# Compressed keys and values of the last three chunks of the sparse branch made in one pass

## The chip, the cores and the metric

The kernel runs on one core of one Trainium2 chip. The metric is the device time of one execution in microseconds (us). All numbers are of the kernel before the change: its runs, and one execution that was profiled.

## The reference

One pre-norm decoder layer: 2048 tokens of width 1024, an input projection of 2700 columns, four attention groups A (stick-breaking), B (native sparse), C (differential) and D (sliding window with sinks), an output projection, an MLP of width 4096 with squared ReLU, and a final norm. The part that the change touches is the compression of group B's keys and values:

```python
def compress(t, pe, w1, w2):                       # 127 windows of 32 tokens, 16 apart, per tensor
    blk = (t[:, idx] + pe).reshape(B, n_cmp, CMP_LEN * t.shape[-1])
    return jax.nn.gelu(blk @ w1) @ w2

kc = compress(k_cmp, pe_k, w1_k, w2_k)
vc = compress(v_cmp, pe_v, w1_v, w2_v)
z = einsum('bthd,bid->bhti', q, kc) * scale - slopes * dist_c     # masked where dist_c < 0
p_c = softmax(z) * valid_c
o_cmp = einsum('bhti,bid->bthd', p_c, vc)
imp = einsum('bhti,ij->btj', p_c, to_sel)          # picks 8 blocks of 64 keys: o_sel
o_nsa = g0 * o_cmp + g1 * o_sel + g2 * o_win
...
mix = concat(rmsnorm(o_sb), rmsnorm(o_nsa), o_diff, rmsnorm(o_swa))
x = x + (mix * g_mix) @ w_out
h = rmsnorm(x); u = relu(h @ w_up); x = x + (u * u) @ w_down
return rmsnorm(x)
```

## The kernel before, in words

**Chunks and phases.** The tokens are cut into NC = 4 chunks of 512. There are eight dense phases, one after the other: P0 to P3 (`proj`, the input projection of a chunk; its column groups come in the order of the table ORDER, one list for chunk 0 and one for the rest) and M0 to M3 (`mlp`: output projection, MLP and final norm of a chunk). Results of P go to scratch memory in DRAM: `qk_d`, `v_d`, and `kvc_d` for the 64 key and 64 value columns that are to be compressed (the group "kvcmp").

**Attention.** Beside the dense phases run the four groups of each chunk, in the order A, C, D, B, for chunk 0 to 3 (`scores`, line 1028). They work tile by tile of 128 queries; PSUM and transposes of them have names by group and chunk, such as zD, tD, oD in group D (scores, transposes, products with v). Their outputs, normed, are stored to `mix_d`, and `mlp` loads them as the tile nx, 4 tiles of 128 rows a chunk, for its output projection.

**Who sets the order.** Every engine executes its instructions in the order in which they were issued. `run` (line 1537) has ten generators, which stand for the streams of work: weights, splits of weights into a high and a low part, loads, finals, values, compressions, scores, fills and the dense phases. At each step it takes the first stream that could start on TensorE (PE) without waiting, by a plan of costs that it keeps (`Plan`, line 122). All DMAs are issued by SyncE (SP) through `dma` (line 245), and a DMA that waits for its buffer holds up those behind it. Ten names are counted resources (line 224); of `row`, work buffers of 128 x 1024 float32, there are RB = 7, and a stream waits until enough are free.

**Compression.** `compressions` (line 1212) makes the 32 compressed keys and values of chunk c when `scores` arrives at group D of that chunk (`compress_due`); group B of the chunk waits for it (`compressed`, line 1294). `compress(c)` (line 1219) takes 3 rows for as long as it runs: `tmp` and, for key (j = 0) and value (j = 1), one that holds the source from `kvc_d`, on 128 partitions (64 columns of two successive half windows), and beside it the source plus the positional offsets `pet`, reordered so that position l of all 32 windows lies together (line 1242). The offsets are loaded with 4 bytes an element. Then come two rounds of two more rows for the weights `w1t`; in each, 8 positions l, a matmul for key and one for value:

```python
for j in range(2):
    self.mm(ph[64 * j:64 * j + 64], ts[j][:, 32 * l:32 * l + 64],
            w1t[j][:, 128 * l8:128 * l8 + 128], l == 0, l == 15, share=2)
```

The stationary operand is 64 columns wide, of which 32 are windows of this chunk; key and value write the two halves of PSUM's partitions. In the order below such a matmul stands as zD<-row 64x128. After it come GELU on a 128 x 128 tile, a transpose, a small product for the keys (into `kcs`, as a high and a low part) and one for the values (into `vcn`). The lists name the same buffers `row` throughout.

Of the kernel before, what the change touches and what calls it, by code (L numbers as in the profile page):

```python
# [9 lines left out]
F32 = mybir.dt.float32  # L10
F32R = mybir.dt.float32r
U32 = mybir.dt.uint32
AF = mybir.ActivationFunctionType
OP = mybir.AluOpType
# [51 lines left out]

# [131 lines left out]
class Trunk:  # L198
# [1013 lines left out]
    def compressions(self):  # L1212
        for c in range(NC):
            while self.compress_due <= c:
                yield None
            yield from self.compress(c)
            self.compressed = c + 1

    def compress(self, c):


        V, A = self.V, self.A
        yield from self.await_stored("kvcmp", c)
        tmp, *ts = yield from self.rows(3)
# [4 lines left out]
        for j in range(2):  # L1229
            t = ts[j]  # L1230
            src = t[:, 512:1024]
            if c:
                self.ld(src[0:64], self.kvc_d[64 * j:64 * j + 64, 512 * c - 16:512 * c + 496])
            else:
                V.memset(src[0:64, 0:16], 0.0)
                self.ld(src[0:64, 16:512], self.kvc_d[64 * j:64 * j + 64, 0:496])
            self.ld(src[64:128], self.kvc_d[64 * j:64 * j + 64, 512 * c:512 * c + 512])
            self.ld(w2t[j], dap(w2s[j], 0, [[64, 128], [1, 64]]))
# [27 lines left out]
        A.activation(xh, ph, AF.Copy)  # L1266
        V.tensor_tensor(u, xh, xh, OP.mult)
        V.tensor_scalar(u, u, 0.044715, 1.0, op0=OP.mult, op1=OP.add)
        V.tensor_tensor(u, u, xh, OP.mult)
        V.tensor_scalar(u, u, -2.0 * math.sqrt(2.0 / math.pi), 80.0, op0=OP.mult, op1=OP.min)  # L1270
        A.activation(u, u, AF.Exp)
        V.tensor_scalar(u, u, 1.0, None, op0=OP.add)
        V.reciprocal(u, u)
        V.tensor_tensor(xh, xh, u, OP.mult)
        yield self.when([xh], "t", TB)
        pT = self.tt()[:, 0, :]
        self.tr(pT, xh)
        self.evac(xT, pT)
        cs = slice(32 * c, 32 * c + 32)
        yield self.z_when(xT)  # L1280
# [7 lines left out]
        A.activation(self.vcn[cs, :], pv[0:32, 0:64], AF.Copy)  # L1288
        self.give_rows(3)

    def sparse(self, c, pa):
# [330 lines left out]
```

## Time and profile before

| what | value |
|---|---|
| median of 3 runs | 3118.82 us (3118.58 to 3120.22) |
| the profiled execution, its own time | 3114.77 us |
| its span on the core | 3113.0 us, 51339 instructions |
| PE, PE's weight loads | 3010.9 us (97%), 2518.6 us (81%) |
| VectorE (DVE), ScalarE (ACT), GpSimd (POOL) | 1852.3 us (60%), 1563.6 us (50%), 498.8 us (16%) |
| DMA | 566.88 MB, 413690 packets, mean 182 GB/s |

How to read it: the share of busy time is of the span. Matmuls are pipelined, so a record lasts longer than the distance from its start to the next one's; what PE spends on one is that distance. PEld are the weight loads, which lie beside PE's matmuls. The clock is what was granted of 2.4 GHz.

### The profile page before, as it was taken

The numbers are of one execution on the slowest core, as the hardware profiler recorded it, in microseconds if no ns is written. First come the engines' busy times: TensorE is split into PE (matmuls) and PEld (weight loads), VectorE is DVE, ScalarE is ACT, GpSimd is POOL, SyncE is SP. The second block draws the span as 40 slices with busy tenths as digits, with TensorE's granted clock in tenths as the row PEclk, the third lists the DMA queues.
The fourth block names the chain that finished last, engine by engine and source line by source line (L and its number), as shares of the span: only waits on it lengthen the run. The fifth ranks groups of instructions, "written<-read, shape, count | busy, mean of one in ns | idle before, by whom it ended". The sixth has DMA issues, their size and how long they took to land.

```text
span 3113.0 us, 51339 instructions
## 1 busy us (share of the span) xinstructions
PE 3010.9 (97%) x19088; PEld 2518.6 (81%) x19088; DVE 1852.3 (60%) x4157; ACT 1563.6 (50%) x3204; POOL 498.8 (16%) x445
## 2 busy tenths in 40 slices
PE   8999998999999999999999999999999999999998
PEld 7878887888887778878888778879888888888887
DVE  4764667655667887684656776677545553332323
ACT  4754667644656775653646775455434343221111
POOL 3142322323212222230100000011000000110000
PEclk9999999999999999999999999999999999999999
DMA  7768565668366667867235446556743333645554
GB/s 212 197 179 216 155 173 144 191 169 259 135 209 208 200 216 250 253 220 243 96 133 161 139 136 193 172 176 204 209 162 124 124 137 137 237 163 203 183 208 157
DMA packets 413690, 566.88 MB, mean 182 GB/s; under 512 B 132864, under 2 KB 300928, under 8 KB 411776
## 3 DMA queue, kind: packets, MB, share of 16 engines
q1 hardware_dynamic: 413440, 563.60, 56.9%
q8 instruction: 151, 2.47, 0.3%
q14 instruction: 99, 0.81, 0.1%
HBM read 434.41 MB, written 129.07 MB: 181 GB/s over the span
## 4 chain that ended last, share of the span: by engine, by line
PE 73%; DVE 10%; ACT 6%; DMA 5%; issue 3%; SPq 2%; POOL 1%; DVEq 0%; ACTq 0%; POOLq 0%
PE pdM L296 43%; PE pdP L296 9%; DVE row L117 7%; ACT row L117 4%; PE tB L300 4%; PE zB L296 4%; PE oB L296 4%; PE oC L296 2%; PE tC L300 2%; PE zC L296 2%; SPq L252 2%; DVE acc L117 1%; DMA raw<-in_w_in_dram 1%; PE zD L296 1%; PE oA L296 1%
## 5 line engine op out<-in xcount | busy, mean ns | idle before, releaser
L117 DVE TENSOR_TENSOR acc<-acc,pdM 128x512 f32<-128x512 f32 (+1 forms) x576 | 371.1, 653 | 193.7 <-PE pdM L296 184.4
L296 PE MATMUL pdM<-T_hi,w_hi 128*128 128x512 f32 (+1 forms) x936 | 357.6, 383 | 2.7 <-ACT T_hi L117 1.9
L296 PE MATMUL pdM<-T_lo,w_hi 128*128 128x512 f32 (+1 forms) x936 | 358.1, 383 | 1.6 <-POOL T_lo L117 1.6
L296 PE MATMUL pdM<-T_hi,w_lo 128*128 128x512 f32 (+1 forms) x936 | 357.8, 382 | 0.0
L296 PE MATMUL pdM<-w_hi,u_hi 128*128 128x512 f32 x776 | 310.9, 403 | 10.4 <-DVE acc L117 5.6
L296 PE MATMUL pdM<-w_hi,u_lo 128*128 128x512 f32 x776 | 305.7, 394 | 3.8 <-DVE u_lo L117 3.8
L296 PE MATMUL pdM<-w_lo,u_hi 128*128 128x512 f32 x776 | 305.9, 394 | 0.9 <-POOL w_lo L117 0.9
L117 POOL TENSOR_TENSOR w_lo<-raw,w_hi 128x1024 fp32r<-128x1024 f32 (+2 forms) x92 | 225.0, 2449 | 408.9 <-ACT w_hi L117 335.2
L117 ACT ACTIVATE row<-row 128x1024 f32<-128x1024 f32 (+7 forms) x292 | 229.7, 802 | 108.2 <-DVE row L117 101.7
L117 ACT ACTIVATE r<-pdM 128x512 f32<-128x512 f32 x128 | 76.1, 594 | 381.4 <-PE pdM L296 370.1
L117 DVE TENSOR_TENSOR u_lo<-r,u_hi 128x512 fp32r<-128x512 f32 x128 | 93.2, 728 | 285.0 <-ACT u_hi L117 285.0
L117 ACT ACTIVATE w_hi<-raw 128x1024 fp32r<-128x1024 f32 (+2 forms) x160 | 164.7, 1036 | 108.6 <-DMA raw<-in_w_in_dram 48.5
L117 ACT ACTIVATE PT<-tB 128x512 f32<-128x512 f32 (+1 forms) x244 | 130.5, 556 | 170.3 <-PE tB L300 169.5
L117 ACT ACTIVATE row<-row,c_mn 128x1024 f32<-128x1024 f32 (+4 forms) x192 | 171.5, 895 | 87.0 <-DVE c_mn L117 85.2
L296 PEld LDWEIGHTS pdM<-T_hi,w_hi 128*128 128x128 f32 x936 | 175.8, 188 | 35.7 <-ACT T_hi L117 2.3
L296 PEld LDWEIGHTS pdM<-T_lo,w_hi 128*128 128x128 f32 x936 | 176.1, 188 | 34.1 <-POOL T_lo L117 2.1
L296 PEld LDWEIGHTS pdM<-T_hi,w_lo 128*128 128x128 f32 x936 | 176.1, 188 | 32.0 <-issue 0.5
L296 PE MATMUL pdM<-raw,u_hi 128*128 128x512 f32 x496 | 190.0, 391 | 0.0
L296 PE MATMUL pdP<-T_hi,w_hi 128*128 128x512 f32 x480 | 189.8, 395 | 0.0
L296 PE MATMUL pdP<-T_hi,w_lo 128*128 128x512 f32 x480 | 189.1, 394 | 0.0
L296 PE MATMUL pdP<-T_lo,w_hi 128*128 128x512 f32 x480 | 189.0, 394 | 0.0
L296 PEld LDWEIGHTS pdM<-w_hi,u_hi 128*128 128x128 f32 x776 | 146.1, 189 | 46.0 <-DVE acc L117 10.3
(222 smaller groups left out, 7124.8 us busy)
## 6 DMA issues: line engine op xcount, KB each, us to landing
w_hi<-w SPq DMA_DIRECT2D x162, 512.0 KB, 3.6
w_lo<-w SPq DMA_DIRECT2D x162, 512.0 KB, 4.9
raw<-w SPq DMA_DIRECT2D x108, 512.0 KB, 4.4
raw<-in_w_in_dram SPq DMA_DIRECT2D x72, 512.0 KB, 4.9
w<-w_hi SPq DMA_DIRECT2D x72, 512.0 KB, 2.9
w<-w_lo SPq DMA_DIRECT2D x72, 512.0 KB, 4.1
acc<-in_x_dram SPq DMA_DIRECT2D x32, 512.0 KB, 4.8
raw<-in_w_up_dram SPq DMA_DIRECT2D x32, 512.0 KB, 5.9
```

Source lines behind the costliest of these rows:

```text
L117: return f(*a, **k)
L252: self.nc.sync.dma_start(dst, src)
L296: self.nc.tensor.matmul(out, a, b, start=start, stop=stop, **k)
L300: self.nc.tensor.transpose(out, a, self.ident[:a.shape[0], :a.shape[0]])
```

## The change

The group kvcmp comes second in the list of chunks 1 to 3 (it was twelfth). `compress` makes chunk 0 alone. A new `compress_rest`, started where chunk 1's compression was, at group D of chunk 1, makes the 96 windows of chunks 1 to 3: it computes all 128, and keeps columns 32 to 127. Keys come first, then values; for each, the source is loaded and offset in two halves of 1024 tokens, and 16 matmuls with 128 stationary columns follow (zD<-row 128x128 in the order). GELU is the same, once on 256 columns. For chunks 2 and 3 `compressions` now does nothing. A pass holds at most five rows.

```diff
@@ -61,8 +61,8 @@
 }
 ORDER = (["vA", "qA0", "qA1", "kA0", "kA1", "qC0", "qC1", "kC0", "kC1", "vC",
           "qB0", "qB1", "kvcmp", "kB", "qD0", "qD1", "kD", "vBD"],
-         ["vA", "qA0", "qA1", "kA0", "kA1", "qC0", "qC1", "kC0", "kC1",
-          "qB0", "qB1", "kvcmp", "kB", "vBD", "qD0", "qD1", "kD", "vC"])
+         ["vA", "kvcmp", "qA0", "qA1", "kA0", "kA1", "qC0", "qC1", "kC0", "kC1",
+          "qB0", "qB1", "kB", "vBD", "qD0", "qD1", "kD", "vC"])
 
 
 def dap(t, off, dims):
@@ -1213,14 +1213,15 @@
         for c in range(NC):
             while self.compress_due <= c:
                 yield None
-            yield from self.compress(c)
+            if c < 2:
+                yield from (self.compress_rest if c else self.compress)()
             self.compressed = c + 1
 
-    def compress(self, c):
+    def compress(self):
 
 
         V, A = self.V, self.A
-        yield from self.await_stored("kvcmp", c)
+        yield from self.await_stored("kvcmp", 0)
         tmp, *ts = yield from self.rows(3)
         xh, u, xT = tmp[:, 0:128], tmp[:, 128:256], tmp[:, 256:384]
         w2t = [tmp[:, 384:448], tmp[:, 448:512]]
@@ -1229,12 +1230,9 @@
         for j in range(2):
             t = ts[j]
             src = t[:, 512:1024]
-            if c:
-                self.ld(src[0:64], self.kvc_d[64 * j:64 * j + 64, 512 * c - 16:512 * c + 496])
-            else:
-                V.memset(src[0:64, 0:16], 0.0)
-                self.ld(src[0:64, 16:512], self.kvc_d[64 * j:64 * j + 64, 0:496])
-            self.ld(src[64:128], self.kvc_d[64 * j:64 * j + 64, 512 * c:512 * c + 512])
+            V.memset(src[0:64, 0:16], 0.0)
+            self.ld(src[0:64, 16:512], self.kvc_d[64 * j:64 * j + 64, 0:496])
+            self.ld(src[64:128], self.kvc_d[64 * j:64 * j + 64, 0:512])
             self.ld(w2t[j], dap(w2s[j], 0, [[64, 128], [1, 64]]))
             for b in range(2):
                 self.ld(pet[j][64 * b:64 * b + 64, :], dap(pes[j], b * 16 * 64, [[1, 64], [64, 16]]))
@@ -1264,19 +1262,12 @@
             self.give_rows(2)
         self.plan.held.discard(z.tensor.name)
         A.activation(xh, ph, AF.Copy)
-        V.tensor_tensor(u, xh, xh, OP.mult)
-        V.tensor_scalar(u, u, 0.044715, 1.0, op0=OP.mult, op1=OP.add)
-        V.tensor_tensor(u, u, xh, OP.mult)
-        V.tensor_scalar(u, u, -2.0 * math.sqrt(2.0 / math.pi), 80.0, op0=OP.mult, op1=OP.min)
-        A.activation(u, u, AF.Exp)
-        V.tensor_scalar(u, u, 1.0, None, op0=OP.add)
-        V.reciprocal(u, u)
-        V.tensor_tensor(xh, xh, u, OP.mult)
+        self.gelu(xh, u)
         yield self.when([xh], "t", TB)
         pT = self.tt()[:, 0, :]
         self.tr(pT, xh)
         self.evac(xT, pT)
-        cs = slice(32 * c, 32 * c + 32)
+        cs = slice(0, 32)
         yield self.z_when(xT)
         pk = self.zt()
         self.mm(pk[0:64, 0:32], w2t[0], xT[:, 0:32], True, True)
@@ -1287,6 +1278,82 @@
         self.mm(pv[0:32, 0:64], xT[:, 64:96], w2t[1], True, True)
         A.activation(self.vcn[cs, :], pv[0:32, 0:64], AF.Copy)
         self.give_rows(3)
+
+    def gelu(self, x, u):
+        V, A = self.V, self.A
+        V.tensor_tensor(u, x, x, OP.mult)
+        V.tensor_scalar(u, u, 0.044715, 1.0, op0=OP.mult, op1=OP.add)
+        V.tensor_tensor(u, u, x, OP.mult)
+        V.tensor_scalar(u, u, -2.0 * math.sqrt(2.0 / math.pi), 80.0, op0=OP.mult, op1=OP.min)
+        A.activation(u, u, AF.Exp)
+        V.tensor_scalar(u, u, 1.0, None, op0=OP.add)
+        V.reciprocal(u, u)
+        V.tensor_tensor(x, x, u, OP.mult)
+
+    def compress_rest(self):
+
+        V, A = self.V, self.A
+        yield from self.await_stored("kvcmp", NC - 1)
+        pes, w1s, w2s = (self.cmp_pe_k, self.cmp_pe_v), (self.cmp_w1_k, self.cmp_w1_v), (self.cmp_w2_k, self.cmp_w2_v)
+        z = None
+        tmp, = yield from self.rows(1)
+        xh, u, xT = tmp[:, 0:256], tmp[:, 256:512], tmp[:, 512:768].rearrange("p (j n) -> p j n", j=2)
+        w2t = [tmp[:, 768:832], tmp[:, 832:896]]
+        for j in range(2):
+            self.ld(w2t[j], dap(w2s[j], 0, [[64, 128], [1, 64]]))
+        for j in range(2):
+            src, *ts = yield from self.rows(3)
+            pet = tmp[:, 896 + 16 * j:912 + 16 * j]
+            for b in range(2):
+                self.ld(pet[64 * b:64 * b + 64, :], dap(pes[j], b * 16 * 64, [[1, 64], [64, 16]]))
+            for h in range(2):
+                kv = self.kvc_d[64 * j:64 * j + 64, :]
+                if h:
+                    self.ld(src[0:64], kv[:, 1008:2032])
+                else:
+                    V.memset(src[0:64, 0:16], 0.0)
+                    self.ld(src[0:64, 16:1024], kv[:, 0:1008])
+                self.ld(src[64:128], kv[:, 1024 * h:1024 * h + 1024])
+                for g in range(2):
+                    V.tensor_tensor(ts[g].rearrange("p (l n) -> p l n", l=8)[:, :, 64 * h:64 * h + 64],
+                                    src.rearrange("p (n l) -> p l n", l=16)[:, 8 * g:8 * g + 8, :],
+                                    pet[:, 8 * g:8 * g + 8, None].to_broadcast([128, 8, 64]), OP.add)
+            self.give_rows(1)
+            w1t = yield from self.rows(2)
+            for g in range(2):
+                for b in range(2):
+                    self.ld(w1t[g].rearrange("p (l j) -> p l j", l=8)[64 * b:64 * b + 64],
+                            dap(w1s[j], (b * 16 + g * 8) * 64 * 128, [[128, 64], [64 * 128, 8], [1, 128]]))
+            for g in range(2):
+                for l8 in range(8):
+                    if z is None:
+                        yield self.z_when(ts[g], w1t[g])
+                        z = self.zt()
+                        self.plan.held.add(z.tensor.name)
+                    else:
+                        yield self.when([ts[g], w1t[g]])
+                    self.mm(z[:, 128 * j:128 * j + 128], ts[g][:, 128 * l8:128 * l8 + 128],
+                            w1t[g][:, 128 * l8:128 * l8 + 128], g + l8 == 0, g + l8 == 8)
+                self.give_rows(2)
+        self.plan.held.discard(z.tensor.name)
+        A.activation(xh, z[:, 0:256], AF.Copy)
+        self.gelu(xh, u)
+        yield self.when([xh], "t", TB)
+        pT = self.tt()
+        for j in range(2):
+            self.tr(pT[:, j, :], xh[:, 128 * j:128 * j + 128])
+        self.evac(xT, pT[:, 0:2, :])
+        yield self.z_when(xT)
+        p = self.zt()
+        self.mm(p[0:64, 0:128], w2t[0], xT[:, 0, :], True, True)
+        A.activation(self.kcs[0:64, 32:128], p[0:64, 32:128], AF.Copy)
+        V.tensor_tensor(self.kcs[64:128, 32:128], p[0:64, 32:128], self.kcs[0:64, 32:128].bitcast(F32), OP.subtract)
+        yield self.z_when(xT)
+        p = self.zt()
+        self.mm(p[:, 0:64], xT[:, 1, :], w2t[1], True, True)
+        for a, b in ((32, 64), (64, 128)):
+            A.activation(self.vcn[a:b, :], p[a:b, 0:64], AF.Copy)
+        self.give_rows(1)
 
     def sparse(self, c, pa):
         V, A = self.V, self.A
```

**PE at group D of chunk 1.** The second half of the compression's matmuls (zD<-row); pdM<-.. T are the output projection of M0, pdM<-identr,nx its transposes, pdP the last projection. Before:

```order
L296 MATMUL oD_8373<-PT,v 64x128 x4
L296 MATMUL zD_8322<-row 64x128
L296 MATMUL oD_8373<-PT,v 64x128 x4
L300 MATMUL tD_8389<-identr,row 128x128 x4
L296 MATMUL pdM_10277<-w_hi,T_lo 128x256
L296 MATMUL zD_8322<-row 64x128 x15
L296 MATMUL pdM_10277<-w_lo,T_hi 128x256
```

In the change, where these are the 16 matmuls of the values:

```order
L300 MATMUL tD_8346<-identr,oS 128x128 x2
L296 MATMUL oD_8361<-PT,v 64x128 x8
L296 MATMUL zD_8282<-row 128x128 x9
L296 MATMUL zD_8480<-kst,qst 128x256 x4
L296 MATMUL zD_8282<-row 128x128 x5
L300 MATMUL tD_8381<-identr,oS 128x128 x2
L300 MATMUL tD_8512<-identr,row 128x128 x4
L296 MATMUL zD_8282<-row 128x128 x2
L300 MATMUL pdM_10495<-identr,nx 128x128 x4
L296 MATMUL pdM_10503<-w_hi,T_hi 128x256
```

The first 16 (keys) stand 45 rows ahead in the change. The transposes of the last nx tile (pdM_10495) now come behind the values' matmuls; before, all of them stood ahead of the second half.

**SP's queue between these two halves.** In the change:

```order
L252 DMA qst<-qk_qD_107 64x2x256
L252 DMA mix_d<-onC 128x64
L252 DMA nx<-mix_d 128x1024
L252 DMA row<-kvc_d 64x1008
L252 DMA row<-kvc_d 64x1024
L252 DMA nat_vC<-u_lo 128x256
L252 DMA mix_d<-onC 128x64
L252 DMA row<-in_cmp_w_v_dram 64x8x128 x2
L252 DMA row<-kvc_d 64x1024 x2
L252 DMA row<-in_cmp_w_v_dram 64x8x128 x2
L252 DMA nx<-mix_d 128x1024
```

Before, the four weight loads of the second half stood here behind both nx loads, and the sources had been loaded before:

```order
L252 DMA mix_d<-onC 128x64
L252 DMA nx<-mix_d 128x1024
L252 DMA nat_vC<-u_lo 128x256 x2
L252 DMA nx<-mix_d 128x1024
L252 DMA v<-nat_vBD 128x8x64
L252 DMA w_10036<-w_hi 128x1024
L252 DMA w_10036<-w_lo 128x1024
L252 DMA row<-in_cmp_w_k_dram 64x8x128 x2
L252 DMA row<-in_cmp_w_v_dram 64x8x128 x2
L252 DMA raw<-in_w_out_dram 128x4x256
```

**SP's queue where M0 ends and group D of chunk 2 begins.** Before:

```order
L252 DMA mix_d<-onC 128x64
L252 DMA kst<-qk_kB 64x1024
L252 DMA out_dram<-acc 128x512
L252 DMA row<-in_cmp_w_k_dram 64x8x128 x2
L252 DMA row<-in_cmp_w_v_dram 64x8x128 x2
L252 DMA out_dram<-acc 128x512
L252 DMA nx<-mix_d 128x1024
L252 DMA out_dram<-acc 128x512 x4
L252 DMA acc<-in_x_dram 128x1024
L252 DMA v<-nat_vBD 128x8x64
L252 DMA qst<-qk_qD_106 64x2x256 x3
L252 DMA mix_d<-onC 128x64
```

In the change:

```order
L252 DMA qst<-qk_qD_106 64x2x256 x4
L252 DMA qst<-qk_qD_107 64x2x256 x4
L252 DMA nx<-mix_d 128x1024 x2
L252 DMA v<-nat_vBD 128x8x64
L252 DMA mix_d<-onC 128x64
L252 DMA out_dram<-acc 128x512 x2
L252 DMA acc<-in_x_dram 128x1024
L252 DMA qst<-qk_qB_103 64x2x256 x4
L252 DMA qst<-qk_qB_104 64x2x256 x4
L252 DMA kst<-qk_kB 64x1536 x2
L252 DMA mix_d<-onC 128x64
L252 DMA kst<-qk_kA_97 64x2048 x2
```

The loads from in_cmp and kvc_d (18 in this passage before, 10 of them ahead of these rows or behind them) are gone, and the two nx loads stand ahead of the output's stores, behind eight loads of q for D.

## Rows read from the trace of the kernel before

**Rows 1.** The page: busy time by engine; chain that ended last, by engine.
```profile
PE 3010.9 (97%) x19088; PEld 2518.6 (81%) x19088; DVE 1852.3 (60%) x4157; ACT 1563.6 (50%) x3204; POOL 498.8 (16%) x445
...
PE 73%; DVE 10%; ACT 6%; DMA 5%; issue 3%; SPq 2%; POOL 1%; DVEq 0%; ACTq 0%; POOLq 0%
```

**Rows 2.** Stretches: from:to, length, busy PE PEld DVE ACT POOL, clock, DMA share, GB/s.
```profile
700.00:760.00 60.00, 54.10 (x487) 51.44 (x486) 30.52 (x91) 29.05 (x74) 23.27 (x17) 0.94 0.80 257
1380.00:1430.00 50.00, 38.72 (x325) 33.30 (x324) 31.69 (x96) 20.41 (x60) 13.42 (x15) 0.93 0.85 252
2080.00:2110.00 30.00, 25.48 (x178) 21.90 (x179) 26.63 (x67) 14.40 (x36) 9.98 (x10) 1.00 0.59 206
...
730.00:740.00 10.00, 9.39 (x93) 8.75 (x94) 2.85 (x8) 6.02 (x11) 7.90 (x6) 0.96 1.13 330
1400.00:1410.00 10.00, 6.55 (x58) 6.05 (x59) 5.88 (x22) 4.32 (x16) 3.14 (x4) 0.83 0.97 306
1420.00:1430.00 10.00, 6.80 (x43) 6.53 (x44) 3.96 (x11) 0.99 (x4) 0.00 (x0) 0.83 0.89 356
```

**Rows 3.** Timeline of PE: start, length, engine, line, operation, out<-in, [idle before <-releaser].
```profile
723.41 1.92 PE L296 MATMUL zD<-row 128*64 128x128 f32 x32
727.84 1.09 PE L300 MATMUL pdM<-identr,nx 128*128 128x128 f32 x4 [2.52 <-DMA nx<-mix_d]
...
738.99 1.93 PE L296 MATMUL zD<-row 128*64 128x128 f32 x30 [0.61 <-DMA row<-in_cmp_w_v_dram]
...
741.64 1.09 PE L296 MATMUL oD<-PT,v 128*64 128x128 f32 x16
...
750.24 0.53 PE L296 MATMUL zD<-row 128*64 128x32 f32 x4
...
1403.45 0.90 PE L300 MATMUL pdM<-identr,nx 128*128 128x128 f32 x3 [3.78 <-DMA nx<-mix_d]
...
1417.75 1.93 PE L296 MATMUL zD<-row 128*64 128x128 f32 x30 [0.56 <-DMA row<-in_cmp_w_v_dram]
1423.20 0.51 PE L296 MATMUL pdM<-raw,T_hi 128*128 128x256 f32 x2 [3.52 <-DMA raw<-w]
...
2230.56 0.43 PE L296 MATMUL zD<-row 128*64 128x128 f32 x2 [0.61 <-DMA row<-in_cmp_w_k_dram]
```

**Rows 4.** Timeline of PE, group B, chunk 3; weight loads by form.
```profile
2512.70 0.72 PE L296 MATMUL zB<-kcs,qst 128*128 128x128 f32 x5
...
L296 PEld LDWEIGHTS pdM<-T_hi,w_hi 128*128 128x128 f32 x936 | 175.8, 188 | 35.7 <-ACT T_hi L117 2.3
```

**Rows 5.** Timeline of SP: start, length of the issues.
```profile
1410.03 1.28 SPq L252 DMA_DIRECT2D row<-in_cmp_w_k_dram  x2
...
1412.09 0.57 SPq L252 DMA_DIRECT2D mix_d<-onC  x1
...
1416.26 0.43 SPq L252 DMA_DIRECT2D raw<-w  x1
```

**Rows 6.** Timeline of DVE at chunk 2's compression.
```profile
1387.72 1.03 DVE L117 TENSOR_TENSOR row<-row 128x512 f32<-128x512 f32 x1 [1.12 <-DMA row<-in_cmp_pe_k_dram]
```

**Rows 7.** DMA issues by size: count, KB each, median us to landing.
```profile
row<-in_cmp_w_v_dram SPq DMA_DIRECT2D x16, 256.0 KB, 5.7
```

**Rows 8.** Pieces of the chain that ended last: start, us, what.
```profile
583.31 4.35 PE pdP L296 x19
...
723.08 4.63 DMA nx<-mix_d
...
730.74 8.11 DMA row<-in_cmp_w_v_dram
...
1395.17 7.08 DMA out_dram<-acc
```

**Rows 9.** Tile qk_qA, 150 to 520 us: lengths in ns, starts.
```profile
L252 SPq DMA_DIRECT2D qst<-qk_qA x16: 573/600/1048, 390.7 to 464.4; - x16
L252 SPq DMA_DIRECT2D qk_qA<-u_hi x4: 320/330/475, 203.7 to 394.7; - x4
```

## The prediction

> **What bounds the kernel now.** I read the page first. TensorE (PE) is busy 97% of the span and holds 73% of the chain that ended last; of VectorE (DVE) it is 10%, of the DMAs 5% [rows 1]. So the time is PE's work plus the moments in which PE stands still, and work taken off another engine is worth nothing unless PE waits for it. Then I looked by stretches for where PE stands still. Two places concern this change. In 1380 to 1430 us PE is busy 38.72 of 50 us, and its mean clock is 0.93 of full [rows 2]. There the MLP of chunk 0 ends, that of chunk 1 begins, and group D's scores and the compression of chunk 2 run. The same passage one chunk later, 2080 to 2110 us, has no compression beside it: PE loses 30 - 25.48 = 4.5 us there, at clock 1.00. In 700 to 760 us (the last projections, the first MLP, D and the compression of chunk 1) PE loses 5.9 us at clock 0.94, and the DMA engines are at their limit: 330 GB/s and a share of 1.13 from 730 to 740 us [rows 2]. The timeline of PE then shows by name which instruction waited for what [rows 3].
>
> **The change part by part.**
>
> *PE work.* One old compression has 32 matmuls 64 columns wide, and a trace record for each of their two fp32 passes: 64. They run in two halves of 32 records, 1.92 us for the first, of which 0.27 us is the last record's own length [rows 3]. So 16 pairs take about 1.76 us, 0.11 us a pair: the key's and the value's half run side by side. A compression is 32 pairs, 3.5 us, plus four records of the two small products, 0.53 us [rows 3], and one transpose at 0.11: 4.15 us; three are 12.4 us. The new pass has 32 matmuls 128 columns wide, again with two records each: 64 steps of 128 moving columns. The trace has no full-width fp32 product. Its nearest row is a full-width matmul of 128 columns with other weights each time: five in 0.72 us, less a last 0.27, 0.11 us a step [rows 4]. So 64 x 0.11 = 7.0, the two products 4 x 0.11 = 0.45, two transposes 0.2: 7.7 us. PE gains **4.7 us**. The other bound is that each weight load shows, 0.188 us [rows 4]: 64 x 0.19 = 12.2, in all 12.8, a loss of 0.4. I take the first, since that row too has a weight load of its own at each step.
>
> *Chunk 2's passage.* Here one compression's loads leave SP's queue, in which every transfer stands in program order: 18 of them, at about 0.6 us each [rows 5]. The order shows the two queues: today 18 issues of the compression stand among nx, the output stores and the weights; then none does. Behind them PE waited 3.78 us for nx (the rows of mix), 0.56 for the value's weights and 3.52 us for raw, the first weights of the MLP [rows 3]; raw was issued at 1416.26, right after the last loads of the compression [rows 5]. DVE stood 1.12 us behind the positional offsets [rows 6]. What stays are the passage's own waits. I price them by the passage of the next chunk, 4.5 us: 11.3 - 4.5 = **6.8 us** gained. Bounds: 2 us (raw alone comes earlier, by the 3 us or so of the last four loads, and the rest stays) and 11.3 (no idle is left).
>
> *The clock there.* After the wait of 3.78 us the mean clock is 0.83 in 1400 to 1410, and after that of 3.52 us again 0.83 in 1420 to 1430 [rows 2]: PE ran part of each slice at 1.2 instead of 2.4 GHz, and each lost up to 1.7 us of full-clock time. The next passage had 1.00. Gain between 0 and 3.4; I take the middle, **1.7 us**, since PE also waited for the other engines while it was slow. The Trainium skill (TensorE: Matmul & The Clock Gate, on HAM oscillation) says that matmul work which is broken by waits for transfers comes back at the half clock and pays half of the throttled time each time. By that rule the two stretches pay 3.4, and the sum below would be 11.5 instead of 9.8.
>
> *Chunk 3.* PE waited 0.61 us for its weights [rows 3]: **0.6 us** gained. But D's scores of chunk 3 now fall on the passage at 2080 us (the order of PE has them between its transposes of nx, formerly some 130 rows later). D has little work for PE to fill gaps with. I charge **1 us**, with bounds 0 and the 4.5 us that this passage loses today, once more.
>
> *Chunk 1.* The stage takes over everything. Its DMAs go from 18 to 22. The sizes: 8 loads of 256 KB from kvc_d (64 partitions x 1024) in place of 4 of half that, 1.6 MB more; the weights are the same 8 x 256 KB [rows 7]. At 330 GB/s [rows 2] that is 4.8 us of a stage whose DMAs are already at their limit. What matters is the second half. Keys go first; only when PE has done their 16 matmuls do the rows come free into which the values' source and weights load. These are 8 loads, with two stores of others among them: ten issues at about 0.6 us [rows 5], so the last is issued 6.0 us later and lands 5.7 (median) [rows 7] to 8.11 us (this stage's own) [rows 8] after that: 11.7 to 14.1 us. PE's cover, between the key's last and the value's first matmul in the new order, is 33 matmuls of 256 columns, 14 transposes for the attention and 12 of nx, 16 products with v, which the trace shows as 32 records, and 4 scores: at 0.12 for 256 columns (half of the 0.23 that 512 take [rows 8]), 0.11 a transpose, and 1.09 for 16 records [rows 3], some 9.5 us: 33 x 0.12 + 26 x 0.11 + 2.18 + 4 x 0.12 = 9.5. So PE waits 2.2 to 4.6 us where it waited 0.61. I charge **3 us**. Bounds: 2 us gained (today's 2.52 for nx goes, as its load now stands ahead of these) and 9 us lost. The four new additions per tensor on DVE (1.03 us each, as [rows 6]) cost nothing while DVE is busy 30.52 of 60 us [rows 2]; without that cover they would add some 2 us to the same wait.
>
> *Order of the projections.* kvcmp moves ahead of ten groups in chunks 1 to 3. No matmul is added. Those groups come one group, 24 matmuls, later: 19 of them take 4.35 us [rows 8], so 24 take 5.5. The reader to fear for is group A of chunk 1: q is stored from 203.7 us on and first read at 390.7 [rows 9]. Stored 5.5 us later, it still has over 180 us, and kvc_d comes earlier. I cost it at nothing; the other work of PE in those 180 us covers it, and without it the whole 5.5 us would show once. ScalarE's and DVE's smaller count (GELU once at 256 columns for three times at 128) is hidden behind PE and counts nothing.
>
> **Sum:** 4.7 + 6.8 + 1.7 + 0.6 - 1 - 3 = 9.8 us less. Against the profiled execution's own 3114.77 us (its span is 3113.0) that is 3105.0. The median of the runs, 3118.82, stands 4.05 above that execution, so I predict **3109.0 us**. A measurement of this kernel can tell about 0.2%, 6.2 us, from no change: faster means under 3112.6, slower over 3125.1.
>
> **The rivals.**
> 1. *The passage keeps its idle time.* The stores of the output and the reloads of x stay where they are at 1390 to 1420 us, and the nx loads now stand behind eight loads for D in SP's queue. For it: out<-acc alone took 7.08 us to land in the chain [rows 8]. Against: the next passage, with the same stores, loses 4.5 only. Then 4.7 + 0.6 - 1 - 3 = 1.3 remain: 3117.5, the same. Chance 0.27.
> 2. *The clock pays whole.* The waits of chunk 2 go and with them all of its slow stretches, and in chunk 1 the wait of 2.52 us for nx and the slow part behind it (0.94 over 60 us: 3.6 us) too. Then 9.8 + 1.7 + 3.6 = 15.1: 3103.7. The page named above would have it so. Against: the new wait at the values may set it back by itself. Chance 0.15.
> 3. *Slower: PE stands at the values' first matmul.* 2.1 MB are asked for at once. With half of 330 GB/s, the other half taken by the output weights and their stores, they need 12.7 us on top of 6.0 of issuing, 18.7 against 9.5 of cover: 9.2 us, and the transposes of the last nx tile, whose load stands behind them in SP's queue, add up to 4.63 us, what that load took [rows 8], and 1.7 for the clock: 15.5 in place of 3. Alone this gives 3109.0 + 12.5 = 3121.5; it decides for slower when it meets rival 1 (then 12.5 - 1.3 = 11.2 lost: 3130.0), that is, from a stand of about 10.5 us on if the passage gains nothing. Chance 0.13.
> That the change doesn't do what it says speaks from no row: the order holds one pass less two, and 32 loads fewer on SP.
>
> **How the numbers follow.** The forecast (gain of 6.2 to 12 us) has 0.45, rivals 1 to 3 have 0.27, 0.15, 0.13. Faster is forecast plus rival 2, 0.60; same is rival 1, 0.27; slower 0.13. The range reaches over rival 2 by a little, to 3101, for the passage's last idle, and over rival 1 up to 3120, to leave out rival 3 and the ends of the others, some 0.2.
>
> **What would show it.** Right: no load of the compression after 760 us; PE's busy time down by 4 to 6 us; at the passage of chunk 2 no wait for raw over 1 us and a clock of 1.00; one wait of 2.2 to 4.6 us at the values' first matmul in chunk 1. Wrong: idle of 8 us or more at the passage without any compression; a wait of over 10 us in chunk 1; steps of the wide matmuls near 0.19 us.

## The result and the profile after

| kernel | median of its runs | ratio to the kernel before, 95% interval |
|---|---|---|
| before, the runs beside the change's | 3118.70 us (3114.70 to 3122.92, 6 runs) | |
| the change | 3098.57 us (3093.30 to 3102.26, 6 runs) | 0.9934 [0.9921, 0.9947] |
| the change, a second time | 3100.15 us (3094.65 to 3101.88, 5 runs) | 0.9942 [0.9930, 0.9955] |

The two ratios are 20.6 us [16.5 to 24.6] and 18.1 us [14.0 to 21.8] of 3118; I use 19.3. The forecast was 9.8 us less, and 3101 to 3120 us as a range: the direction was right, the size half of what came, and the time 2.4 us under the range.

The two profiled executions (before 3114.77, after 3102.26 us) stand only 12.5 apart: the one of before was among its fast ones, the one of after the slowest of six. So places are read from the profiles here, and sizes from the medians.

The page of the change (span; busy time; chain by engine), against [rows 1]:

```profile
span 3100.0 us, 51033 instructions
...
PE 2999.9 (97%) x18951; PEld 2519.8 (81%) x18951; DVE 1852.9 (60%) x4145; ACT 1565.3 (50%) x3195; POOL 507.2 (16%) x445
...
PE 78%; DVE 8%; ACT 5%; DMA 5%; issue 2%; POOL 1%; SPq 1%; DVEq 0%; POOLq 0%; ACTq 0%
```

PE's busy time fell by 11.0 us, where the forecast had 4 to 6. Its idle time, which is the span less the busy time, fell only from 102.1 to 100.1 us. A second profile of each kernel (below) gives 3.5 us of busy time and 7.9 of idle, so one pair of profiles does not split the gain to better than some 7 us. The same three stretches as in [rows 2], in the change:

```profile
700.00:760.00 60.00, 51.46 (x440) 48.13 (x439) 36.52 (x106) 28.52 (x79) 21.13 (x18) 0.94 0.89 263
1380.00:1430.00 50.00, 45.99 (x347) 39.97 (x345) 39.67 (x136) 34.65 (x100) 17.90 (x18) 0.97 0.95 286
2080.00:2110.00 30.00, 27.47 (x206) 24.23 (x201) 24.02 (x62) 15.56 (x35) 6.16 (x8) 1.00 0.81 263
```

The passage of chunk 2 loses 50 - 45.99 = 4.0 us (11.3 before; the forecast left 4.5) at clock 0.97, where the prediction's sign of being right was 1.00. The next one loses 2.5 where it lost 4.5, with D's scores of chunk 3 now in it. The stage of the pass loses 8.5 us (5.9 before). PE's timeline there, and in the passage:

```profile
718.60 2.72 PE L296 MATMUL zD<-row 128*128 128x128 f32 x22
722.14 0.33 PE L300 MATMUL tC<-identr,oS 128*128 128x128 f32 x1 [0.82 <-ACT oS L117]
722.74 1.28 PE L296 MATMUL zD<-row 128*128 128x128 f32 x10
...
729.41 0.66 PE L300 MATMUL pdM<-identr,nx 128*128 128x128 f32 x4 [2.53 <-DMA nx<-mix_d]
...
740.00 4.21 PE L296 MATMUL zD<-row 128*128 128x128 f32 x18 [3.07 <-DVE row L117]
744.86 1.42 PE L296 MATMUL zD<-row 128*128 128x128 f32 x10
...
1389.77 0.59 PE L296 MATMUL zD<-kst,qst 128*128 128x256 f32 x3 [0.96 <-DMA qst<-qk_qD]
...
1412.21 0.30 PE L296 MATMUL zB<-kcs,qst 128*128 128x128 f32 x1 [1.46 <-DMA qst<-qk_qB]
```

A wide step takes (1.28 - 0.275) / 9 = 0.11 us (0.275, a record's own length, stands in the group below), as forecast. At 740.00 it takes (4.21 - 0.42) / 17 = 0.22: PE had stood for 3.07 us, and those 18 run at half clock (0.42 is a record's length there, and the clock granted from 740 to 744 us is 0.50). The wait for nx is still there, 2.53 us after 2.52 [rows 3], where the prediction's better bound and its rival 2 had it gone. No wait for raw is left in the passage.

The matmuls zD<-row by count, in the change and in the kernel before (min, median and longest in ns, first and last start, forms):

```profile
L296 PE MATMUL zD<-row x136: 219/275/582, 258.1 to 771.2; 128*64 128x128 f32 x66, 128*128 128x128 f32 x64, 128*64 128x32 f32 x2, 128*32 128x64 f32 x2
```

```profile
L296 PE MATMUL zD<-row x272: 219/273/413, 256.8 to 2269.0; 128*64 128x128 f32 x128, 128*64 128x32 f32 x4, 128*32 128x64 f32 x4
```

Half of them are gone, and none stands after 772 us.

### The profile page after: what moved, and what is told of

It reads as the page before. It is cut to its first block, busy times and chain, and to the rows that moved or that the text cites. A ratio compares the mean times of both kernels' runs of the same rounds, so it can differ in the third digit from the quotient of the medians.

```text
span 3100.0 us, 51033 instructions
## 1 busy us (share of the span) xinstructions
PE 2999.9 (97%) x18951; PEld 2519.8 (81%) x18951; DVE 1852.9 (60%) x4145; ACT 1565.3 (50%) x3195; POOL 507.2 (16%) x445
## 4 chain that ended last, share of the span: by engine, by line
PE 78%; DVE 8%; ACT 5%; DMA 5%; issue 2%; POOL 1%; SPq 1%; DVEq 0%; POOLq 0%; ACTq 0%
PE pdM L296 45%; PE pdP L296 10%; DVE row L117 5%; PE zB L296 4%; PE tB L300 4%; PE oB L296 4%; ACT row L117 3%; PE zC L296 2%; PE oC L296 2%; PE tC L300 2%; DVE acc L117 1%; DMA raw<-in_w_in_dram 1%; PE oA L296 1%; PE tA L300 1%; PE zA L296 1%
## 5 line engine op out<-in xcount | busy, mean ns | idle before, releaser
L117 ACT ACTIVATE row<-row,b_mw 128x640 f32<-128x640 f32 (+7 forms) x160 | 134.5, 842 | 93.9 <-DVE b_mw L117 93.5
```

The costliest lines, as they stand in the source:

```text
L117: return f(*a, **k)
```

## Experiments

The question is where the 9.5 us come from that the sum by parts lacks. First, is it the pass or the new place of kvcmp in the list? And does a list alone move this kernel, whose order is planned anew with every edit?

**The list alone.** The kernel before with

```diff
-"vA", "qA0", ..., "qB0", "qB1", "kvcmp", "kB"
+"vA", "kvcmp", "qA0", ..., "qB0", "qB1", "kB"
```

> The kernel before with the new list alone (kvcmp second in chunks 1 to 3), every chunk still compressed by itself. Theory A (the pass makes the gain, the order is worth nothing): 3118.7 +- 4 us. Theory B (the earlier projection is what gains, since the compression's loads come free earlier): 3112 us or less, the waits of chunk 2's passage (3.78 and 3.52 us) gone. Theory C (any new plan moves the time by some us, whatever was changed): off by more than 4 us on either side, with the differences spread over stretches in which nothing is compressed.

Measured: 3119.82 us, ratio 1.0003 [0.9994, 1.0012]. The list gains nothing by itself, as the prediction had it. Theory B falls.

**The pass alone**, under the old list (the diff above, reversed, in the changed kernel).

> The changed kernel with the old list (kvcmp twelfth), so the pass alone. The pass must wait for the keys and values of chunk 3, whose projection now comes ten groups later. Theory A: 3098.6 +- 4 us, as the change itself. Theory B: 3105 us or more. Theory C: anywhere from 3095 to 3115 us.

Measured: 3106.22 us, ratio 0.9959 [0.9946, 0.9973]: 12.8 us less by the ratio, 11.9 by the medians. Neither A's 3098.6 nor plainly B's loss, since the list alone gave nothing: it fits C.

**Two neighbours swapped**, in the kernel before:

```diff
-"kvcmp", "kB", "vBD", "qD0"
+"kvcmp", "vBD", "kB", "qD0"
```

> The kernel before with two neighbours of the list, kB and vBD, swapped in chunks 1 to 3: no work added or taken away, nothing of the compression touched. Theories A and B: 3118.7 +- 3 us. Theory C: off by more than 4 us.

Measured: 3124.81 us, ratio 1.0023 [1.0014, 1.0033]: 7.2 us slower, with no work changed. Its nine runs had mean clocks of 0.988 to 0.991, those of before beside them 0.991 to 0.995. A difference of 0.003 is 9 us of full-clock time, so the clock alone could be all of it. The page says otherwise:

```profile
core 0: 3123.1 us, clock 0.990
...
PE 3012.4 (96%) x19088; PEld 2523.6 (81%) x19088; DVE 1864.0 (60%) x4157; ACT 1567.0 (50%) x3204; POOL 507.1 (16%) x445
```

PE is busy 1.5 us longer than in the profile of before and stands still 110.7 us instead of 102.1. So most of it is waits.

**Another swap**, of the queries and keys of group A (kA0, kA1 ahead of qA0, qA1).

> The kernel before with the queries and keys of group A swapped in the list of chunks 1 to 3 (kA0, kA1 ahead of qA0, qA1); the compression as before. The swap of kB and vBD cost 7 us though it added no work. If that was the reading order of those two groups, this one stays within 3 us of 3118; if any new plan moves the time by some us, it is off by 3 to 8 on either side.

Measured: 3109.91 us, ratio 0.9976 [0.9965, 0.9987]: 7.5 us faster, at clocks of 0.990 to 0.993, so here it is not the clock either. PE stands still 94.4 us, 7.7 less than before, and is busy 2.0 longer:

```profile
core 0: 3107.3 us, clock 0.991
...
PE 3012.9 (97%) x19088; PEld 2526.4 (81%) x19088; DVE 1850.1 (60%) x4157; ACT 1563.7 (50%) x3204; POOL 506.5 (16%) x445
```

These two new plans are worth some 7 us, one either way, and both through PE's waits. My range had no term for that.

**The change under these two lists.**

> The changed kernel with kB and vBD swapped, as in n1_swap. If the change gains its 19 to 20 us whatever the list, this is 3124.8 - 20 = 3105 +- 3. If the change itself is worth the 10 to 13 us of the sum by parts and the rest was the luck of one plan, 3112 to 3116.

> The changed kernel with group A's queries and keys swapped, as in n2_swap. Gain fixed: 20 us under n2_swap, +- 3. Gain of 10 to 13 plus luck: between 5 and 20 us under it, and not the same as for the other swap.

Measured: 3100.15 and 3101.68 us. The change gains 24.7 under the first swap and 8.2 under the second; with the two lists of the diff it gains 19.3 (old list before, new list after) and, old list on both sides, 11.9. Its own four times lie in 3099 to 3106, those of the kernel before in 3110 to 3125: means 3101.9 and 3118.2, 16.3 apart. Under the same list on both sides the four gains are 11.9, 20.4, 24.7 and 8.2, which leaves their mean uncertain by some 4 us (standard error). So some 16 us, give or take 4, belong to the change, and the rest to the plans it was compared under.

**The compressions left out, one by one and together** (kernel before):

```diff
-            yield from self.compress(c)
+            if c < 2:
+                yield from self.compress(c)
```

(with c != 2 and c != 3 for one alone)

> The kernel before with the compressions of chunks 2 and 3 left out (their compressed keys and values stay zero). It shows what these two cost, loads, waits and matmuls together. Theory A by the prediction's terms: 2 x 4.15 us of PE work, 6.8 of the passage, 1.7 of the clock, 0.6 of chunk 3: 17.4 less, 3101.3 us. Theory A with a compression at the 4.65 to 5.02 us that the trace of before shows for the PE time of these two when the change-overs to and from other work are counted (0.37 and 0.75 more to get into them): 10.8 + 9.1 = 19.9 less, 3098.8 us. Theory C: less than 12 us, as what is taken out here comes back elsewhere.

> The kernel before without the compression of chunk 2 alone (its compressed keys and values stay zero). By the prediction's terms it costs 4.15 us on PE + 6.8 in the passage + 1.7 of the clock = 12.7: 3105.5 us. By the trace of the kernel without both, read at equal work, the stage gains 12.3: 3105.8. If the passage keeps its idle (rival 1), 5 us: 3113.

> The kernel before without the compression of chunk 3 alone. By the prediction's terms 4.15 + 0.6 = 4.75 us: 3113.4. If the two together cost 22.8 because chunk 3 costs more than I charged, 8 to 10 us: 3109 us.

Measured: both 3095.34 us (22.8 less), chunk 2 alone 3116.47 (ratio 0.9995 [0.9986, 1.0004], nothing), chunk 3 alone 3103.70 (13.7 less). They don't add: 15.3 against 22.8. Without chunk 2's compression the passage itself does gain, then the plan that follows is another one. Stretches of that kernel:

```profile
1380.00:1430.00 50.00, 44.60 (x355) 40.88 (x354) 36.02 (x134) 27.03 (x85) 10.35 (x13) 0.93 0.91 279
2080.00:2110.00 30.00, 30.00 (x228) 27.79 (x229) 23.99 (x63) 14.43 (x33) 2.19 (x4) 1.00 0.88 303
```

It loses 5.4 in the passage (11.3 before) and nothing in the next, yet the gain is gone by the end: over the whole span PE is busy 3010.7 us and idle 103.2, both as before. Its eleven runs had mean clocks of 0.990 to 0.993, and 0.001 of the span is 3 us of full-clock time. One plan against another is no price.

**The loads kept, the work left out** (chunks 2 and 3):

```diff
+            if c > 1:
+                self.give_rows(2)
+                continue
             for l8 in range(8):
...
+        if c > 1:
+            self.give_rows(3)
+            return
```

> The kernel before where the compressions of chunks 2 and 3 issue all their loads and add the offsets, but their matmuls, GELU and products are left out. If the loads make the waits of the passage (prediction: 6.8 + 1.7 + 0.6 for them), only PE's own work of two compressions goes, 8.3 to 10.8 us: 3108 to 3110 us. If the loads are harmless and the waits come from PE's own place in the order, nearly all of the 22.8 goes: 3096 us.

Measured: 3109.89 us, ratio 0.9977 [0.9966, 0.9987]: 7.2 less of the 22.8. The forecast for harmful loads was 3108 to 3110. PE's idle time is 105.5 us with the loads and 95.2 without them, so most of what these two cost seems to hang on their loads, as the prediction argued; the plan differs between the two as well, so the shares are rough.

**The plan held.** To get prices, I let the planner go through a compression as before, with every cost charged and every row held, but issue none of its instructions:

```diff
+    def planned_only(self, g):
+        while True:
+            self.plan.ghost = True
...
+            yield r
...
-        self.nc.tensor.matmul(out, a, b, start=start, stop=stop, **k)
+        if self.plan.ghost:
+            self.nc.get_next_instruction_name()
+        else:
+            self.nc.tensor.matmul(out, a, b, start=start, stop=stop, **k)
```

and the same for transposes, DMAs and the other engines. By its code `run` then makes the same choices to the last step. But `run` is not the last to set the order, as it seemed ahead of the prediction: the library's scheduler orders the instructions once more, so the executed order is held only in part. Counted in the traces as the fewest DMAs that must move to get the order of SP's 1768 in the kernel before, 102 stand elsewhere when chunks 2 and 3 are planned and not issued, 213 for chunk 1 and 196 for all three. Simply leaving chunks 2 and 3 out moves 120, and the two swaps move 300 and 253. The pass planned and not issued moves 213 against the change. So these prices, too, have some of a new order in them.

> The kernel before in which the compressions of chunks 2 and 3 are planned as before (their costs are charged and their rows held) but none of their instructions is issued, so that the plan of all other work is the one of before. The compressed keys and values of these chunks stay zero. By the prediction's terms for the two, 8.3 of PE + 6.8 + 1.7 + 0.6 = 17.4 less: 3100.5 us; with PE's 10.8 as measured, 19.9: 3098. If half of the 22.8 that leaving them out gained came from the new plan, 3106 us.

> The kernel before in which the compression of chunk 1 is planned but not issued. It prices the old compression where the pass now stands. By the prediction's terms 4.15 of PE + 0.61 of wait, with 2.52 for nx if that goes as well: 4.8 to 7.3, 3110.5 to 3113 us. If the old one cost as much as the new pass, 11 or more: 3106.5 us; then the pass came at no price and the change's gain is that of the two that went, 15.5, and some luck.

> The kernel before in which the compressions of chunks 1, 2 and 3 are planned but not issued (their compressed keys and values stay zero). If the prices add, 15.5 + 11.6 = 27.1 less: 3090.7 us, and within 3 us of the changed kernel without its pass (3088.8). If each price was in part the luck of its own order, 18 to 22 less: 3096 to 3100 us, and the order of the list would be worth 7 us or more by itself.

> The changed kernel in which the pass of chunks 1 to 3 is planned (costs charged, rows held) but none of its instructions is issued; the compressed keys and values of these chunks stay zero. It prices the pass. By the prediction's terms 7.7 of PE + 3 of waits = 10.7: 3099.4 - 10.7 = 3088.7 us. By the trace (7.5 to 7.9 of PE, 3.07 of wait, 2.1 of half clock, 1.3 less for chunk 0) 12 to 13: 3087 us. If the pass is nearly free because its place is filled with waits anyway, 4 to 6: 3094 us.

| left out, the plan held | median, us | ratio to before | us of 3118 | forecast |
|---|---|---|---|---|
| chunks 2 and 3 | 3101.31 | 0.9945 [0.9932, 0.9957] | 17.1 [13.4 to 21.2] | 17.4 |
| chunk 1's old compression | 3106.34 | 0.9964 [0.9952, 0.9977] | 11.2 [7.2 to 15.0] | 4.15 (with waits, ahead of the run: 4.8 to 7.3) |
| all three | 3089.51 | 0.9909 [0.9894, 0.9924] | 28.4 [23.7 to 33.0] | 21.5 |
| the pass, from the change | 3088.78 | 0.9904 [0.9889, 0.9919] | 29.9; less the change's 19.3: 10.6 | 10.7 |

The prices add: 17.1 + 11.2 = 28.3 against 28.4; with intervals of 4 us on each, that they meet to 0.1 is luck. And the two kernels without any compression after chunk 0 lie within 0.7 us of each other by the medians and 1.5 by the ratios, although one has the old list and one the new: these two lists are worth about the same. The gain is 28.4 - 10.6 = 17.8; the 1.5 left of 19.3 are that difference of the two kernels, which is within the noise.

The old compression of chunk 1 is the price that I had wrong. Its stage without it:

```profile
700.00:760.00 60.00, 56.97 (x492) 53.25 (x491) 33.70 (x117) 32.47 (x80) 20.76 (x17) 0.97 0.73 235
```

PE loses 3.0 us there instead of 5.9 [rows 2], and the longest wait of the stage before is gone, which the prediction's rows and its sum did not have:

```profile
703.21 0.39 PE L296 MATMUL pdP<-w_hi,T_hi 128*128 128x256 f32 x1 [2.77 <-ACT w_hi L117]
```

In the kernel before, the chain that ended last reaches this wait through the compression: its positional offsets are awaited, DVE adds them, the weight loads of its first half follow in SP's queue (692.75), and only behind these is the load of the projection's weight (raw) issued that w_hi is made of:

```profile
685.10 2.74 DMA row<-in_cmp_pe_k_dram
...
687.96 2.44 DVE row L117
...
692.75 1.41 SPq L252
...
695.58 6.45 DMA raw<-in_w_in_dram
...
702.11 1.06 ACT w_hi L117
```

Without this compression the chain stays on PE from 680 to 705 us. Over the whole span more goes than in the stage:

```profile
core 0: 3101.6 us, clock 0.992
...
PE 3008.3 (97%) x19019; PEld 2516.1 (81%) x19019; DVE 1836.5 (59%) x4147; ACT 1568.0 (51%) x3199; POOL 506.1 (16%) x445
```

PE's idle time is 93.3 us, 8.8 less than before, and its busy time 2.6 less (9.4 less and 0.1 more than in the second profile of before, below). So the price is waits for the most part, and two thirds of them lie outside the stage.

The passage of chunk 2 with its compression planned and not issued:

```profile
1380.00:1430.00 50.00, 40.89 (x325) 34.01 (x325) 36.70 (x146) 30.92 (x94) 14.15 (x17) 0.93 0.88 255
```

Here 9.1 us of idle stay in the stretch that I said would gain 6.8, with other waits (q of D, q of B, raw). Nor does as much idle time go elsewhere:

```profile
core 0: 3099.6 us, clock 0.992
...
PE 2998.4 (97%) x18950; PEld 2514.1 (81%) x18950; DVE 1840.3 (59%) x4137; ACT 1561.3 (50%) x3194; POOL 500.1 (16%) x445
```

PE's idle time over the span is 101.2 us, 0.9 less than before, and its busy time 12.5 less. So the total of the two came out right, but not by the waits that the prediction took off.

**A second profile of the kernel before**, unchanged.

> The kernel before once more, for a second profile. If the waits of chunk 2's passage belong to the kernel, 1380 to 1430 us again loses 10 to 13 us; if to the execution, less than 8. The same for the 5.9 us of 700 to 760.

```profile
700.00:760.00 60.00, 53.03 (x500) 50.30 (x501) 30.88 (x94) 30.66 (x81) 23.21 (x17) 1.00 0.81 263
1380.00:1430.00 50.00, 40.03 (x341) 34.89 (x340) 31.50 (x102) 19.78 (x60) 12.07 (x14) 0.93 0.86 261
2080.00:2110.00 30.00, 26.88 (x195) 23.82 (x194) 24.80 (x63) 14.25 (x34) 9.96 (x10) 1.00 0.66 223
```

```profile
core 0: 3110.9 us, clock 0.995
...
PE 3008.2 (97%) x19088; PEld 2516.9 (81%) x19088; DVE 1853.2 (60%) x4157; ACT 1562.5 (50%) x3204; POOL 498.9 (16%) x445
```

It loses 10.0 us in the passage (again 0.93) and 7.0 in chunk 1's stage: the waits belong to the kernel. Its idle time over the span is 102.7 us (102.1 in the first profile). In chunk 1's stage they show one by one, and the compression's own weights cost 1.54 + 0.66, where the execution that I priced from had 0.61 [rows 3]:

```profile
701.80 0.39 PE L296 MATMUL pdP<-w_hi,T_hi 128*128 128x256 f32 x1 [2.45 <-ACT w_hi L117]
...
725.65 0.63 PE L300 MATMUL pdM<-identr,nx 128*128 128x128 f32 x4 [2.67 <-DMA nx<-mix_d]
...
734.84 0.29 PE L296 MATMUL zD<-row 128*64 128x128 f32 x1 [1.54 <-DMA row<-in_cmp_w_k_dram]
...
737.03 1.93 PE L296 MATMUL zD<-row 128*64 128x128 f32 x30 [0.66 <-DMA row<-in_cmp_w_v_dram]
```

**The change a second time.**

> The changed kernel once more, for a second profile of it: 3098.6 +- 2 us in the median. If the clock makes the difference between executions, its time follows the mean clock: about 3 us for each 0.001 of it. In the first profile the stage between equal work 1050 and 1125 us had lost 5 us to a half-clock stretch and waits in chunk 1's groups A and C; if that belongs to the kernel, it is here again, and if to the execution, it is gone.

Measured: 3100.15 us; its profile again loses in 700 to 760 (53.46 of 60 busy) and little in the passage (46.49 of 50), so these belong to the kernel. So does a loss that I had not foreseen, where groups A and C of chunk 2 begin. The first and the second profile there:

```profile
1100.00:1200.00 100.00, 92.73 (x541) 73.74 (x542) 77.39 (x138) 62.09 (x113) 24.58 (x13) 0.97 0.65 208
```

```profile
1100.00:1200.00 100.00, 93.18 (x543) 74.11 (x542) 78.48 (x138) 61.89 (x113) 24.46 (x13) 0.97 0.66 210
```

The kernel before, in its first profile:

```profile
1100.00:1200.00 100.00, 98.39 (x592) 78.38 (x590) 78.53 (x147) 69.08 (x123) 27.08 (x15) 1.00 0.73 230
```

The change gives back some 5 us here, in a stretch in which nothing is compressed. In the 100 us ahead of it PE stands still less than before (6.4 and 3.8 us against 7.6), so of the 5 us 4.5 and 1.5 are left over 1000 to 1200 us. Its five runs do follow the clock: 3094.65 us at 0.992, 3097.68 at 0.991, 3100.15 and 3101.50 at 0.990, 3101.88 at 0.989, some 2.4 us for each 0.001. The six of the first set do not (3093.30 and 3102.26 both at 0.992).

**The pass's own wait.** The chain of the change at the values:

```profile
731.81 1.02 DVE row L117
...
732.84 0.47 SPq L252
...
733.41 4.57 DMA row<-kvc_d
...
738.07 1.88 DVE row L117
...
740.00 6.28 PE zD L296 x32
```

It is not the weights that come last but the second source, which can only be loaded when DVE has offset the first, out of the same row; DVE's additions on it (1.88 us), which the prediction took as covered, stand in the chain as well. So load the values' first source while the keys' matmuls run:

```diff
-            src, *ts = yield from self.rows(3)
+            if src is None:
+                src, *ts = yield from self.rows(3)
+            else:
+                ts = yield from self.rows(2)
...
-            self.give_rows(1)
+            if j:
+                self.give_rows(1)
+            else:
+                self.cmp_source(src, 1, 0)
```

(cmp_source holds the loads of one half; the values' first half is not loaded again.)

> The changed kernel in which the values' first source is loaded into the keys' source row as soon as the keys are offset, so that it arrives while the keys' matmuls run. The pass then holds six rows of seven between the two. If the wait of 3.07 us at the values' first matmul and the half clock behind it are paid in the end, 3 to 5 us less: 3095 us. If the wait moves to the second source and the weights, or the missing row holds up the scores, 3099.4 +- 3; more than that only by a new plan.

> The changed kernel with the values' first source loaded early (v1_early), under the list with kB and vBD swapped. If the earlier source is worth 7 us in itself, it stands 7 us under the changed kernel with that list (3100.2): 3093 us. If 3 to 4 of it were the wait and the rest the plan: 3096 to 3097 us. If all of it was the plan: 3100 +- 3.

Measured: 3091.81 us, ratio 0.9918 [0.9904, 0.9931], the fastest of these kernels that still computes everything, 7.6 us under the change; but with the swapped list 3101.80, 1.6 above the change with that list. In the first the values start without a wait, in the second they still wait (2.21 us, where the change with that list had 2.45):

```profile
751.06 2.50 PE L296 MATMUL zD<-row 128*128 128x128 f32 x20
```

```profile
758.15 1.13 PE L296 MATMUL zD<-row 128*128 128x128 f32 x8 [2.21 <-DVE d_es L117]
```

So whether the early source removes the wait depends on where the plan puts the rest. That the wait is paid in the end fits both runs, but they do not show it apart from the plan: of the 7.6 us the wait and the half clock behind it explain up to 3.07 + 2.

## Why the prediction was right in its direction and wrong in its size

By its own steps, with the sum written by compression (forecast, then measured):

- **Chunks 2 and 3** (two thirds of the PE term's 12.4, the passage, the clock, 0.6): 17.4; measured 17.1 [13.4 to 21.2] with the plan held. Right in the sum, and in part by luck: with these two planned and not issued PE's idle time over the span fell by 0.9 us (1.5 against the second profile of before), where the sum had 7.4 of waits, and its busy time by 12.5 (9.8), where it had 8.3 + 1.7 = 10.0. In the change itself the passage does gain as forecast: it loses 4.0 where I left 4.5, and its clock is 0.97 after 0.93: 50 x 0.04 = 2.0 us, forecast 1.7. The Trainium skill (TensorE: Matmul & The Clock Gate, on HAM oscillation) would have had 3.4: here part of the slow time stayed. But over the whole span PE stands still 100.1 and 94.8 us in the two profiles of the change, 102.1 and 102.7 before, so a good part of the 7.3 saved there is lost again at other places.
- **The pass**: 7.7 on PE and 3 of new wait, 10.7; measured 10.6. A step is 0.11 us as taken from the row with 128 other columns, and the wait 3.07 us. Its cause was another one, the second source and DVE's additions and not the weights, so that the size agrees is luck.
- **Chunk 3 on the next passage**: a charge of 1 us with a bound at 4.5. That passage lost 2.5 in the change, 2 less than before (2.4 against 3.1 in the second profiles). Wrong by 2 to 3 us at the place, in the other direction.
- **The order**: nothing; measured 1.0003.
- **Chunk 1, the step that failed.** I set 4.15 us for the old compression there, its PE work alone, set its own wait of 0.61 against the new one, and took the other waits of its stage as not its own: "Bounds: 2 us gained (today's 2.52 for nx goes, ...)". The longest of them, 2.77 us for w_hi, stands in no term at all. Planned and not issued, the old compression is worth 11.2 [7.2 to 15.0]. For chunk 2 I had put the nx, raw and clock losses down to the compression's loads; in chunk 1 the same kind of loads stood in the same queue ahead of nx and the weights, at the higher DMA share of the two places (1.13 against 0.97 [rows 2]), and I charged them nothing, since the new pass loads more. For w_hi the chain of before shows it; that wait is gone in the change too, the one for nx is not. Of the 7 us between, 2.9 are the idle time that goes from the stage; the other waits lie outside it, where the order differs as well, and their cause stays open. No run kept chunk 1's loads and left its work out.

So the miss of 9.5 is 7 of that step, 1 of the charge for D, and 1.5 of plans, with intervals of 4 us on each price and more on their differences. By the four lists the change is worth 16 +- 4, so 3 of the 9.5 us, give or take 4, can be the plans that it was measured under. The PE term by itself was too small for chunks 2 and 3 as well: added up from the starts in the trace of before, an old compression of chunks 1 to 3 took 4.07, 4.65 and 5.02 us, and 0.37 to 0.75 more in the matmuls ahead of its pieces, in place of 4.15, since it lies in four to eight pieces between other work. In the prices above that is contained.

**The rivals.** The passage did not keep its idle time in the change (rival 1); in the kernel where its compression is planned and not issued it did, for the most part. The clock did not pay whole (rival 2): the change's runs had 0.990 to 0.992, lower than those of before, and gained all the same, so 3103.7 was near for the wrong reason. PE did not stand at the values for over 10 us (rival 3). The range was too narrow also because it had no term for a new plan of everything behind the change: two harmless swaps are worth +7.2 and -7.5 us.

## What to carry to other kernels

Price what is taken out with all the waits of its stage, not only with its busy time, and use the same rule at every place where it stands. Where a planner or a scheduler orders the work anew at each edit, swap two harmless things first to see how much a plan alone moves, put that into the range, and judge a change under several orders. To get the price of a piece, let the planner count it and issue nothing: such prices added here (17.1 + 11.2 against 28.4), those from leaving code out did not (1.6 + 13.7 against 22.8). Then compare busy and idle time over the whole span, since a wait that goes at one place can come back at another: a sum that is right need not be right by its parts.

## What the runs showed of the hardware

More time at half clock need not show in the end. The two profiles of the change have mean clocks of 0.992 and 0.990, some 6 us of full-clock time apart, and spans of 3100.0 and 3099.5 (the last row is the busy time of the second):

```profile
core 0: 3100.0 us, clock 0.992
```

```profile
core 0: 3099.5 us, clock 0.990
```

```profile
PE 3004.7 (97%) x18951; PEld 2526.0 (81%) x18951; DVE 1853.5 (60%) x4145; ACT 1565.5 (51%) x3195; POOL 508.1 (16%) x445
```

In the second PE is busy 4.8 us longer and stands still 5.3 us less (94.8 against 100.1), so its slow time seems to lie in good part where it would otherwise have waited for others. I had counted every slow stretch as a loss. A list that adds no work lowered the mean clock too (n1_swap, 0.988 to 0.991), and there as well PE's busy time grew little (1.5 us against the first profile of before, 4.2 against the second); what cost the time was 8 us more of waits.
